# A decoder layer on one core: where RWKV's gates stand between the triangles and the scan

## The chip, the core and the metric

One core of a Trainium2 chip runs the whole program. TensorE (PE) multiplies, VectorE (DVE), ScalarE (ACT) and GpSimd (POOL) work element by element, SyncE (SP) issues most DMAs, and GpSimd issues the gathers of the experts' rows. The metric is the device time of one execution in microseconds.

## The reference, cut to what matters

One layer of a hybrid decoder over a prompt of 1024 tokens and over 8 sample tokens: a gated mixer (an SSD branch and an RWKV-7 branch), cross attention over 256 memory tokens, and a lookup of experts (each token dots 128 rows of `expert_u` and sums 128 rows of `expert_v`). The change concerns the mixer, and in it the gate of the RWKV branch:

```python
g = jax.nn.sigmoid(gl) @ p['rwkv_g2']
yr, wkv_new = _rwkv7_scan(rh, heads(decay), kh, vh, -kk, kk * ah, wkv_prev)
...
y_rwkv = (yr + bonus.reshape(b, L, D_RWKV)) * g
gate_ssd, gate_rwkv = jnp.split(jax.nn.sigmoid(gate_raw), 2, axis=-1)
merged = gate_ssd * y_ssd + gate_rwkv * y_rwkv
```

The factor g times gate_rwkv is wanted only when the scan's output of a block of 128 tokens is complete.

## The kernel before

The prompt is done in four fronts of two blocks of 128 tokens; `front(gi)` is the mixer of one of them, and what follows (attention, choice of experts) is `rest`. The experts' rows of a finished front are gathered by GpSimd (L1514), dotted (L1518) and summed (L1570) on VectorE beside the next front, so fronts 1 to 3 share VectorE and the DMA engines with that stream, and front 0 doesn't. In front 0 the memory's keys and values are computed beside the scan instead.

Inside a front: norm, projections, convolution and SSD, RWKV's projections, then four stages that matter here.

- **Triangles**: the scan treats chunks of 64 tokens at once, and needs inverses of triangles of 32 x 32. All of a front lie in one tile, and 31 steps on VectorE (a product, L843, and a sum, L845) invert them. The result is written to memory (`td`, L846) and read back by each chunk in another shape (`tx`, L911).
- **SSD gates** (L849 to 857): four strips of 256 columns of w_in. A strip is, for each block, a group of matmuls against 1 MB of weights (two loads at L256) into a PSUM tile pp.
- **RWKV gates** (L860 to 882): four rounds q, each with such a strip per block, tanh on ScalarE (L870), a matmul with rwkv_g2 into a PSUM tile pc, and their product on VectorE (L874) into gg. The front with the sample rows (front 1) has a third strip per round, and loads 8 rows of the sample's result (yr, L880). Read at L1019.
- **Scan**: for each of the two blocks b and each of its two chunks c, scores (pg, pc, with masks at L928 and L930 and transposes tp at L934), the read-back inverse turned (L912) and used (tp from tx), then px, pu (solution), py (outputs), ps, and the state rst (L992, L993), on which the next chunk's px waits. A front has four chunks, counted 0 to 3 below.

In the source the gates stand between the triangles and the scan. A scheduler orders each engine's instructions ahead of time by what they depend on and by their place in the source, so that the gates run on TensorE while VectorE inverts. Weight tiles come from a pool of five halves of a strip; PSUM has two tiles each for pp, pc and tp. All engines run their list strictly in order.

The sample's own experts (products at L1697, matmuls pv) run beside front 3.

Of the kernel before, what the change touches and what calls it, by code (L numbers as in the profile page):

```python
# [29 lines left out]
MPOS = 2  # L30
# [16 lines left out]
def decode_layer(ctx, tc, I, O):  # L47
# [17 lines left out]
    def t(tag, shape, bufs, dt=F32):  # L65
        uid[0] += 1
        return (we if tag in of_experts else pools.get(tag, pools.get("wd", wk))).tile(shape, dt, tag=tag, name=f"{tag}_{uid[0]}", bufs=bufs)
# [4 lines left out]
    def rowt():  # L72
        return t("U", [P, D], n_u())

    def q3():
        return t("q3", [P, 2, TMAX], NQ3)
# [10 lines left out]
    def k1():  # L87
        return t("k1", [P, 256], NK1)

    def f2():  # L90
        return t("f2", [P, 512], 4)
# [5 lines left out]
    def pp():  # L97
        return pst("pp", 2)
# [7 lines left out]
    def pc():  # L106
        return pst("pc", 2)

    def pv():
        uid[0] += 1  # L110
        return psp.tile([P, D], F32, tag="pv", name=f"pv_{uid[0]}", bufs=1)

    def mm(out, a, b, first=True, last=True):
        T.matmul(out, a, b, start=first, stop=last)  # L114

    def copy(out, in_, scale=None, bias=None):
        if bias is not None:
            S.activation(out, in_, AF.Identity, scale=scale if scale is not None else 1.0, bias=bias)
        else:
            S.activation(out, in_, AF.Copy, scale=scale if scale is not None else 1.0)  # L120
# [74 lines left out]
    c = spots["conv_w"]  # L195
# [57 lines left out]
    def weights(w, c0, n=256, split=False):  # L253
        x = Weights()
        for i in range(2):
            load(x.half[i][:, :, :n], w[i * 512:(i + 1) * 512, c0:c0 + n].rearrange("(k p) c -> p k c", p=P))  # L256
        return parts(x) if split else x
# [73 lines left out]
    def by_token(wt, h, t0, n, p, nw=256):  # L331
        for k in range(8):
            if isinstance(h, Parts):
                three(p[:n, :nw], h.of(k, slice(t0, t0 + n)), wt[k], k == 0, k == 7)
            else:
                mm(p[:n, :nw], h[k // 2][:, k % 2, t0:t0 + n], wt.of(k, slice(0, nw)), k == 0, k == 7)
# [127 lines left out]
    def front(gi):  # L464
# [393 lines left out]


        gg = [[q3().rearrange("p j x -> p (j x)") for _ in range(2)] for _ in range(nb)]  # L860
        for q in range(4):
            qs = slice(q * 256, q * 256 + 256)
            g2 = k1()
            load(g2, I["rwkv_g2"][0, :, qs])
            wt = weights(w_in, GR0 + q * 256, split=sa)
            for b, (t0, n) in enumerate(body):
                p = pp()
                by_token(wt, hT, t0, n, p)
                th = f2()
                S.activation(th[:n, :256], p[:n, :256], AF.Tanh, scale=0.5)  # L870
                p2 = pc()
                if b < nb:
                    mm(p2[:, :256], lor[:, 1, t0:t0 + n], g2)
                    V.scalar_tensor_tensor(gg[b][q // 2][:, (q % 2) * 256:(q % 2) * 256 + 256], th[:, :256], 1.0,  # L874
                                           p2[:, :256], op0=OP.add, op1=OP.mult)
                else:
                    mm(p2[:n, :256], smp["gl"], g2)
                    V.scalar_tensor_tensor(th[:n, :256], th[:n, :256], 1.0, p2[:n, :256], op0=OP.add, op1=OP.mult)
                    gy = f2()
                    load(gy[:n, :256], smp["yr"][:, qs])  # L880
                    V.tensor_tensor(gy[:n, :256], th[:n, :256], gy[:n, :256], op=OP.mult)
                    V.tensor_tensor(mg[nb][:n, qs], mg[nb][:n, qs], gy[:n, :256], op=OP.add)
        if gi == 0 and MPOS == 0:
            memory()
            keys()


        lnw = []
# [5 lines left out]
        def scan(b):  # L894
            yq = [q3().rearrange("p j x -> p (j x)") for _ in range(2)]
            for c in range(2):
# [94 lines left out]
                        mm(ps[sl, ac], E[s][a // 4][:, a % 4, 0:64], uv[:, s, ac])  # L991
                V.tensor_tensor(rst, ps.rearrange("p (a v) -> p a v", a=8), rst, op=OP.add)  # L992
                V.tensor_tensor(rst, rst, wc[:, :, ch_:ch_ + 1].to_broadcast([P, 8, 64]), op=OP.mult)  # L993


            gst = t("gst", [P, 2, 16], 2)
# [211 lines left out]
        if gi in SPLIT and ORDER:  # L1208
            res = []
            for b in range(nb):  # L1210
                scan(b)
                if gi == 0 and b == 0 and MPOS:
                    memory()
                    keys()
                res += rest([b])
        else:
            for b in range(nb):
                scan(b)
                if gi == 0 and b + 1 == MPOS:
                    memory()  # L1220
                    keys()
            if last and ORDER == 0:
                final_states()
            res = [x for b in range(nb) for x in rest([b])] if gi in SPLIT else rest(list(range(nb)))
# [481 lines left out]
    def keys():  # L1706
        for i in range(2):
            x = rowt()
            load(x.rearrange("p (x d) -> p x d", x=8),
                 I["sub_keys"][0].rearrange("h c k d -> k (h c) d")[:, i * 8:i * 8 + 8, :])  # L1710
            p = pv()
            for c in range(8):
                T.transpose(p[:, c * P:(c + 1) * P], x[:, c * P:(c + 1) * P], ident)
            o = t("acc", [P, D], NAC)
            copy(o, p)
            load(kt2_d[i], o.rearrange("p (x k) -> p x k", x=8))
# [9 lines left out]

    late = []
    chosen = front(0)
    sample_recurrences()
    for gi in range(1, len(GROUPS)):  # L1730
        ahead = front(gi)
        z = experts(prompts(chosen), GATHERED[gi - 1])
        late += [x for i, x in enumerate(z) if i not in GATHERED[gi - 1]]
        samples(chosen)
        chosen = ahead
# [71 lines left out]
```

## Time and profile before

| | us |
|---|---|
| timed runs, median of 3 | 4762.22 (4757.62 to 4777.23) |
| the profiled execution | 4803.32, its span 4801.6 |
| VectorE busy | 3656.8 (76%) |
| TensorE busy | 3581.8 (75%) |
| fronts' triangles begin | 308, 1249, 2245, 3276 |
| states of chunks 0 to 3 done (L993), front 0 | 397, 430, 469, 505 |
| the same, front 1 | 1377, 1419, 1464, 1497 |
| the same, front 2 | 2354, 2394, 2439, 2471 |
| the same, front 3 | 3390, 3433, 3478, 3522 |

The profiled execution is 0.86% longer than the median of the timed runs. A busy TensorE is not TensorE at its peak: the granted clock, 1.00 for 2.4 GHz and 0.50 for 1.2 GHz, is a column of its own. The stages' limits are not those of the average, so that windows are cut along the times in the table.

### The profile page before, as it was taken

How to read it: one execution, taken by the hardware profiler on the slowest of the kernel's cores; microseconds unless marked ns; L12 is line 12 of the kernel's file. 1: busy time of each engine (PE TensorE's matmuls, PEld its weight loads, DVE VectorE, ACT ScalarE, POOL GpSimd, SP SyncE). 2: the span in 40 equal slices, each digit the busy share in tenths (PEclk: the TensorE clock that was granted, in tenths of full speed). 3: DMA queues.
4: the chain of work that ended last, by engine and by line, in shares of the span. 5: the costliest groups of instructions: out<-in, count | busy, mean ns of one | idle time of the engine just before them, and what ended most of it. 6: DMA issues, size and time to landing. Idle time of an engine off the chain costs nothing.

```text
span 4801.6 us, 56531 instructions
## 1 busy us (share of the span) xinstructions
PE 3581.8 (75%) x18486; PEld 2721.1 (57%) x18486; DVE 3656.8 (76%) x7730; ACT 1345.3 (28%) x3461; POOL 2456.4 (51%) x2059
## 2 busy tenths in 40 slices
PE   7889865769887786687676953588867964089995
PEld 6778764557565674365555742465655623056663
DVE  4662296998878779988786899877773798786775
ACT  5544322123132221232232311231321222143331
POOL 0000044765657644655566567745563566754444
PEclk9988887889856896888668976688578985589997
DMA  4342589899978997999799897999788888889997
GB/s 121 99 140 62 195 285 324 269 319 347 342 256 301 360 345 255 343 331 340 269 312 337 318 322 246 335 296 331 224 314 284 283 290 272 309 285 364 354 363 266
DMA packets 609102, 1369.20 MB, mean 285 GB/s; under 512 B 86124, under 2 KB 332296, under 8 KB 608800
## 3 DMA queue, kind: packets, MB, share of 16 engines
q0 software_dynamic: 260352, 948.03, 55.8%
q1 hardware_dynamic: 348456, 417.57, 26.2%
q8 instruction: 146, 2.39, 0.2%
q14 instruction: 148, 1.21, 0.1%
HBM read 1335.60 MB, written 29.90 MB: 284 GB/s over the span
## 4 chain that ended last, share of the span: by engine, by line
PE 40%; DVE 29%; DMA 11%; issue 10%; ACT 5%; POOL 4%; SPq 1%; another core or an unknown queue 0%; POOLq 0%; DVEq 0%; ACTq 0%
PE pp L114 21%; PE pc L114 10%; DVE U L1518 8%; DVE acc L1570 4%; PE pv L114 4%; POOL U L1514 4%; DMA U<-in_expert_u_dram,idx 3%; DMA U<-in_expert_v_dram,idx 2%; PE pg L114 2%; DVE q3b L452 2%; DVE vs L1618 1%; PE tp L114 1%; DMA w<-in_w_in_dram 1%; DVE f L581 1%; DVE q3b L455 1%
## 5 line engine op out<-in xcount | busy, mean ns | idle before, releaser
L1514 POOL DMA_INDIRECT U<-in_expert_u_dram,idx x1024 | 1280.9, 1251 | 828.9 <-DVE act L1518 249.4
L1518 DVE CUSTOM_DVE_ANT_0 U<-U,xa 128x1024 f32<-128x1024 f32 x1032 | 1271.1, 1239 | 140.8 <-DMA U<-in_expert_u_dram,idx 132.8
L1514 POOL DMA_INDIRECT U<-in_expert_v_dram,idx x768 | 900.7, 1173 | 751.4 <-DVE act L1518 248.0
L1570 DVE SCALAR_TENSOR_TENSOR acc<-U,cf,acc 128x1024 f32<-128x1024 f32 x656 | 863.5, 1316 | 111.4 <-DMA U<-in_expert_v_dram,idx 102.5
L114 PE MATMUL pp<-qw,w 128*128 128x256 f32 (+2 forms) x2872 | 731.3, 407 | 159.6 <-issue 43.8
L114 PEld LDWEIGHTS pp<-qw,w 128*128 128x128 f32 x2872 | 580.6, 214 | 281.8 <-issue 107.3
L114 PE MATMUL pp<-w,qw 128*128 128x256 f32 (+1 forms) x2528 | 623.0, 400 | 116.8 <-ACT f L856 44.5
L114 PEld LDWEIGHTS pp<-w,qw 128*128 128x128 f32 (+1 forms) x2528 | 477.4, 192 | 242.7 <-ACT f L856 46.9
L114 PE MATMUL pv<-U,dg 128*128 128x512 f32 x448 | 240.8, 669 | 99.1 <-DMA U<-in_expert_v_dram,idx 85.6
L114 PEld LDWEIGHTS pv<-U,dg 128*128 128x128 f32 x448 | 88.8, 209 | 217.5 <-issue 147.6
L114 PE MATMUL pc<-vs,cs 128*128 128x512 f32 x510 | 204.3, 455 | 1.9 <-DVE vs L1648 1.9
L114 PE MATMUL pp<-q,w 128*128 128x128 f32 (+1 forms) x1024 | 187.2, 340 | 4.5 <-DMA w<-in_w_pq_dram 3.3
L123 POOL TENSOR_TENSOR q3b<-q3b,q3b 128x400 f32<-128x400 f32 (+1 forms) x130 | 152.1, 1184 | 55.8 <-DVE q3b L452 53.2
L114 PEld LDWEIGHTS pp<-q,w 128*128 128x128 f32 x1024 | 163.3, 202 | 19.1 <-issue 3.7
L114 PE MATMUL pp<-vs,cs 128*128 128x512 f32 x510 | 172.2, 392 | 0.0
L114 PE MATMUL pc<-rst,q 64*64 64x64 f32 x1024 | 170.5, 305 | 2.2 <-issue 1.2
L114 PE MATMUL pg<-q,q 64*128 64x128 f32 (+1 forms) x384 | 110.8, 447 | 71.6 <-DMA q<-kt_d 33.3
L306 PE MATMUL tp<-ident,g 128*128 128x128 f32 (+1 forms) x296 | 60.8, 340 | 138.0 <-DVE g L1020 50.5
L114 PE MATMUL pc<-g,q 128*64 128x64 f32 x1024 | 140.0, 317 | 23.1 <-issue 16.6
L1648 DVE TENSOR_TENSOR vs<-Vx,vs 128x512 fp32r<-128x512 f32 x170 | 111.7, 688 | 42.1 <-ACT vs L120 35.0
L114 PEld LDWEIGHTS pg<-q,q 64*128 64x128 f32 (+1 forms) x384 | 82.5, 276 | 94.1 <-ACT q L1130 40.1
L306 PEld LDWEIGHTS tp<-ident,g 128*128 128x128 f32 (+1 forms) x296 | 43.2, 179 | 157.7 <-issue 56.2
(506 smaller groups left out, 6336.3 us busy)
## 6 DMA issues: line engine op xcount, KB each, us to landing
w<-in_w_in_dram SPq DMA_DIRECT2D x248, 512.0 KB
Vx<-in_expert_v_dram SPq DMA_DIRECT2D x128, 512.0 KB
w<-in_w_pq_dram SPq DMA_DIRECT2D x80, 512.0 KB
w<-in_w_out_dram SPq DMA_DIRECT2D x40, 512.0 KB
w<-in_w_mq_dram SPq DMA_DIRECT2D x40, 512.0 KB
w<-in_w_mo_dram SPq DMA_DIRECT2D x40, 512.0 KB
U<-in_expert_u_dram,idx POOLq DMA_INDIRECT x1024
U<-in_expert_v_dram,idx POOLq DMA_INDIRECT x768
```

The source lines that it names most:

```text
L114: T.matmul(out, a, b, start=first, stop=last)
L123: G.tensor_tensor(out, a, b, op=op)
L306: T.transpose(p[:, j * P:j * P + n], x[:, c * P:(c + 1) * P], ident[:n, :n])
L452: V.tensor_tensor(oh[:n], iota50[:n, None, :].to_broadcast([n, 8, NCAND]), posf[:n, h, k8].unsqueeze(2).to_broadcast([n, 8, NCAND]), op=OP ...
L455: V.tensor_reduce(idf[:n, h, k8], oh[:n], axis=AX.X, op=OP.add)
L581: V.scalar_tensor_tensor(acc[:, 3 - k:TP], p[:, :TP - 3 + k], cw(k), acc[:, 3 - k:TP], op0=OP.mult, op1=OP.add)
L1514: G.indirect_dma_start(out=dst, out_offset=None, in_=table, in_offset=bass.IndirectOffsetOnAxis(ap=idx, axis=0))
L1518: V.tensor_tensor_reduce(out=u, in0=u, in1=x, scale=1.0, scalar=0.0, op0=OP.mult, op1=OP.add, accum_out=out)
L1570: V.scalar_tensor_tensor(z["acc"], v, cf, z["acc"], op0=OP.mult, op1=OP.add)
L1618: V.tensor_scalar(rb[:, a, :], iota, by[:, 1, t0 + a:t0 + a + 1], by[:, 2, t0 + a:t0 + a + 1], op0=OP.is_equal, op1=OP.mult)
L1648: V.tensor_tensor(vl, v[:, s], vh.bitcast(F32), op=OP.subtract)
```

## The change

The loop over q becomes a function `gate_rwkv(q)`, and scan(0), the scan of the first block, calls it at the end of each of its two chunks: q = 0 and 1 behind chunk 0, q = 2 and 3 behind chunk 1. This holds for all fronts. The removed lines on MPOS did nothing (MPOS is 2).

```diff
--- before.py
+++ after.py
@@ -858,7 +858,7 @@
 
 
         gg = [[q3().rearrange("p j x -> p (j x)") for _ in range(2)] for _ in range(nb)]
-        for q in range(4):
+        def gate_rwkv(q):
             qs = slice(q * 256, q * 256 + 256)
             g2 = k1()
             load(g2, I["rwkv_g2"][0, :, qs])
@@ -880,9 +880,6 @@
                     load(gy[:n, :256], smp["yr"][:, qs])
                     V.tensor_tensor(gy[:n, :256], th[:n, :256], gy[:n, :256], op=OP.mult)
                     V.tensor_tensor(mg[nb][:n, qs], mg[nb][:n, qs], gy[:n, :256], op=OP.add)
-        if gi == 0 and MPOS == 0:
-            memory()
-            keys()
 
 
         lnw = []
@@ -991,6 +988,9 @@
                         mm(ps[sl, ac], E[s][a // 4][:, a % 4, 0:64], uv[:, s, ac])
                 V.tensor_tensor(rst, ps.rearrange("p (a v) -> p a v", a=8), rst, op=OP.add)
                 V.tensor_tensor(rst, rst, wc[:, :, ch_:ch_ + 1].to_broadcast([P, 8, 64]), op=OP.mult)
+                if b == 0:
+                    for q in range(2 * c, 2 * c + 2):
+                        gate_rwkv(q)
 
 
             gst = t("gst", [P, 2, 16], 2)
```

Every instruction before exists after; the lists are in another order. In SP's list of front 2, here around the write of the inverse (td), before (w_in and w_out are weights; w_15110 and w_15111 belong to q = 3):

```order
L256 DMA w_15110<-in_w_in_dram 128x4x256
L256 DMA w_15111<-in_w_in_dram 128x4x256
L256 DMA w_16142<-in_w_out_dram 128x4x256
L256 DMA w_16143<-in_w_out_dram 128x4x256
L256 DMA w_16166<-in_w_out_dram 128x4x256
L256 DMA w_16167<-in_w_out_dram 128x4x256
L256 DMA w_16190<-in_w_out_dram 128x4x256
L846 DMA td_188<-g_2839_14822 128x1024
L911 DMA tx_15150<-td_188 32x16x32 x2
```

and of the change (w_15228, w_15229 belong to q = 0, w_15508, w_15509 to q = 2, w_15542, w_15543 to q = 3):

```order
L256 DMA w_15228<-in_w_in_dram 128x4x256
L256 DMA w_15229<-in_w_in_dram 128x4x256
L256 DMA w_15262<-in_w_in_dram 128x4x256
L256 DMA w_15263<-in_w_in_dram 128x4x256
L256 DMA w_15508<-in_w_in_dram 128x4x256
L256 DMA w_15509<-in_w_in_dram 128x4x256
L256 DMA w_15542<-in_w_in_dram 128x4x256
L846 DMA td_188<-g_2839_14822 128x1024
L908 DMA tx_15014<-td_188 32x16x32 x2
L256 DMA w_15543<-in_w_in_dram 128x4x256
L256 DMA w_16142<-in_w_out_dram 128x4x256
```

The five loads of w_out that stood right ahead of the write stand behind it, and weights of q = 2 and half of q = 3 are what stands ahead.

TensorE, front 2, from the last matmul of ps of chunk 0 (pc_15343, after: pc_15207) to chunk 1's scores (pc_15384, after: pc_15316), before:

```order
L114 MATMUL pc_15343<-g_2924_15247,q_2915_15163 64x64
L114 MATMUL pc_15384<-q_2725_14252,q_2726_14253 128x128
L114 MATMUL pc_15384<-q_2727_14261,q_2728_14262 128x128
L114 MATMUL pc_15384<-q_2760_14423,q_2761_14424 128x128
L114 MATMUL pc_15384<-q_2762_14432,q_2763_14433 128x128
L114 MATMUL pg_15399<-q_2795_14594,q_2796_14595 128x128
```

and of the change (pp_15526 is the second strip of q = 2; pc from k_ and q_2657 is the product with rwkv_g2, two blocks each of q = 0 and q = 1):

```order
L114 MATMUL pc_15207<-g_2888_15111,q_2879_15027 64x64
L114 MATMUL pp_15526<-w_15508,qw_12965 128x256 x2
L114 MATMUL pp_15526<-w_15508,qw_12966 128x256 x2
L114 MATMUL pp_15526<-w_15509,qw_12967 128x256 x2
L114 MATMUL pp_15526<-w_15509,qw_12968 128x256 x2
L114 MATMUL pc_15243<-k_2894_15226,q_2657_13949 128x256
L114 MATMUL pc_15257<-k_2894_15226,q_2657_13949 128x256
L114 MATMUL pc_15277<-k_2903_15260,q_2657_13949 128x256
L931 MATMUL tp_15347<-ident,q_2796_14595 128x128
L931 MATMUL tp_15347<-ident,q_2798_14604 128x128
L931 MATMUL tp_15347<-ident,q_2831_14766 128x128
L931 MATMUL tp_15347<-ident,q_2833_14775 128x128
```

A strip and four gate products (the fourth behind these rows) now stand between the two chunks. The strips of q = 0 stay ahead of the scan, the two of q = 1 stand where the inverse is read back, the first of q = 2 between pu and py of chunk 0; chunk 1 has the same with q = 3. In front 1, with three strips a round, three stand at the end of chunk 0, one and a quarter inside chunk 1, and two and three quarters at its end; none is left between the triangles and chunk 0's scores.

VectorE, end of front 0's triangles, before (q_501 and q_503 are gg; L247 is the norm of the memory):

```order
L845 TENSOR_TENSOR g_458_2873<-g_458_2873,f_459_2874 128x2x30
L874 SCALAR_TENSOR_TENSOR q_501_3214<-f_551_3478,pc_3480 128x256
L843 TENSOR_TENSOR f_459_2874<-g_457_2872,g_458_2873 128x31
L247 RECIPROCAL ssm_4481<-ssm_4481 128x1
L845 TENSOR_TENSOR g_458_2873<-g_458_2873,f_459_2874 128x31
L874 SCALAR_TENSOR_TENSOR q_503_3216<-f_554_3508,pc_3510 128x256
L928 TENSOR_TENSOR q_563_3531<-pg_3535,maskg 128x4x64
L930 TENSOR_TENSOR f_562_3530<-pg_3535,maskg 64x256
```

and of the change (U_3809, w_3879 and U_3883 are weights split into two parts, which only front 0 does; L909 to L990 are L912 to L993 of before):

```order
L845 TENSOR_TENSOR g_458_2873<-g_458_2873,f_459_2874 128x2x30
L843 TENSOR_TENSOR f_459_2874<-g_457_2872,g_458_2873 128x31
L845 TENSOR_TENSOR g_458_2873<-g_458_2873,f_459_2874 128x31
L909 STREAM_TRANSPOSE tx_3225<-tx_3225 32x1024
L292 TENSOR_TENSOR U_3809<-w_3800,U_3807 128x1024
L909 STREAM_TRANSPOSE tx_3585<-tx_3585 32x1024
L292 TENSOR_TENSOR w_3879<-w_3873,U_3877 128x1024
L989 TENSOR_TENSOR rst<-pc_3418,rst 128x512
L990 TENSOR_TENSOR rst<-rst,wc_1534 128x512
L292 TENSOR_TENSOR U_3883<-w_3874,U_3881 128x1024
L874 SCALAR_TENSOR_TENSOR q_500_3213<-f_537_3476,pc_3478 128x256
L874 SCALAR_TENSOR_TENSOR q_502_3215<-f_540_3506,pc_3508 128x256
```

The products of gates and the norm are gone from the last steps, and the gates follow the state of chunk 0; the masks of chunk 0 stand ahead of the last steps. Of the splits at L292, 11 stand in front 0's triangles before and 8 after; of the masks, none before and eight after.

VectorE's experts, L1518 and L1570 together, counted in the two lists by stage, before and after ("rest" is all between the scan of the front before and these triangles; the tail is what follows the state of chunk 3 up to the last merge, L1020):

| | rest | triangles | chunk 0 | chunk 1 | chunk 2 | chunk 3 | tail |
|---|---|---|---|---|---|---|---|
| front 1 | 225, 218 | 32, 39 | 20, 18 | 22, 28 | 20, 28 | 17, 17 | 17, 16 |
| front 2 | 306, 316 | 24, 33 | 25, 22 | 19, 20 | 23, 25 | 17, 10 | 17, 14 |
| front 3 | 348, 342 | 24, 14 | 15, 8 | 18, 19 | 19, 21 | 18, 18 | 12, 12 |

The gates' operations on VectorE (L874, and for the sample rows L878, L881, L882) stand, by the same count, before: 7 in the triangles and 1 in chunk 0 (front 1: 8 and 12); after: 4 in chunk 1 and 4 in chunk 2 (front 1: 10 and 10). Behind front 3's scan the counts are the same. The sample's experts (L1697) stand in chunk 0 of front 3 before, and in its triangles after. In front 0 the memory's matmuls that stood inside the scan stand behind it as far as the gates take their places.

## Rows read from the trace of the kernel before

**Rows 1.** Windows of stages named below: columns are named in the first line.

```profile
core 0: us, PE busy (x) PEld busy (x) DVE busy (x) ACT busy (x) POOL busy (x), PEclk, DMA share, GB/s
530.00:575.00 45.00, 32.34 (x210) 27.47 (x208) 7.24 (x23) 14.12 (x38) 0.41 (x2) 0.89 0.81 275
1249.00:1312.00 63.00, 58.23 (x248) 38.75 (x249) 62.27 (x133) 6.09 (x17) 44.82 (x33) 0.93 1.00 367
1312.00:1377.00 65.00, 55.48 (x398) 42.60 (x396) 36.45 (x61) 18.46 (x47) 24.53 (x22) 0.66 0.76 259
1377.00:1419.00 42.00, 37.04 (x306) 29.87 (x304) 36.54 (x45) 12.26 (x42) 31.24 (x26) 0.50 0.76 255
1419.00:1464.00 45.00, 37.58 (x323) 31.13 (x323) 37.05 (x60) 21.59 (x69) 28.26 (x22) 0.50 0.71 236
2298.00:2354.00 56.00, 30.98 (x313) 25.31 (x312) 39.59 (x52) 14.11 (x39) 32.88 (x29) 0.60 0.75 261
2354.00:2394.00 40.00, 30.93 (x296) 24.96 (x296) 31.95 (x43) 13.74 (x48) 24.59 (x22) 0.58 0.76 254
2394.00:2439.00 45.00, 36.26 (x306) 29.75 (x307) 41.12 (x62) 19.02 (x59) 31.50 (x25) 0.50 0.82 267
2439.00:2470.00 31.00, 26.58 (x284) 21.56 (x283) 24.66 (x35) 8.49 (x24) 21.62 (x18) 0.72 0.86 284
3329.00:3390.00 61.00, 55.17 (x369) 35.34 (x368) 34.07 (x46) 18.10 (x46) 27.43 (x26) 0.67 0.74 242
```

**Rows 2.** Groups of instructions: count, busy us, mean ns; or count, ns min/median/max.

```profile
L1518 DVE CUSTOM_DVE_ANT_0 U<-U,xa 128x1024 f32<-128x1024 f32 x1032 | 1271.1, 1239 | 140.8 <-DMA U<-in_expert_u_dram,idx 132.8
...
L1570 DVE SCALAR_TENSOR_TENSOR acc<-U,cf,acc 128x1024 f32<-128x1024 f32 x656 | 863.5, 1316 | 111.4 <-DMA U<-in_expert_v_dram,idx 102.5
...
L874 DVE SCALAR_TENSOR_TENSOR q<-f,pc x32: 406/414/422, 330.5 to 3330.7; 128x256 f32<-128x256 f32 x32
...
L292 DVE TENSOR_TENSOR w<-w,U x31: 1215/1225/1227, 25.4 to 340.1; 128x1024 fp32r<-128x1024 f32 x31
...
L928 DVE TENSOR_TENSOR q<-pg,maskg 128x256 f32<-128x256 f32 x3 | 1.3, 422 | 9.4 <-PE pc L114 9.3
```

**Rows 3.** Timeline of VectorE, end of front 0's triangles: start us, us, [idle before <-releaser].

```profile
351.41 0.42 DVE L874 SCALAR_TENSOR_TENSOR q<-f,pc 128x256 f32<-128x256 f32 x1 [1.90 <-ACT f L870]
...
353.02 0.16 DVE L247 RECIPROCAL ssm<-ssm 128x1 f32<-128x1 f32 x1 [1.09 <-ACT ssm L246]
```

**Rows 4.** Timeline of SP, the inverse's write and read, fronts 0 and 1.

```profile
353.34 0.34 SPq L846 DMA_DIRECT2D td<-g  x1
...
356.38 0.87 SPq L911 DMA_DIRECT2D tx<-td  x2
...
1312.15 0.33 SPq L846 DMA_DIRECT2D td<-g  x1
...
1326.46 1.95 SPq L911 DMA_DIRECT2D tx<-td  x2
```

**Rows 5.** Chain that ended last, 1290 to 1385: start us, us, what.

```profile
by line: PE pc L114 19.2%; DMA f<-yr_d 18.0%; issue 12.1%; DVE acc L1570 11.8%; DMA tx<-td 6.5%; DVE U L1518 4.3%; PE pv L114 4.0%; PE tp L114 3.7%; PE pg L114 3.3%; DVE g L845 3.0%; DVE f L843 2.9%; DVE q L874 2.1%; DVE acc L1535 1.5%; DVE
```

**Rows 6.** Waits of TensorE, 2298 to 2358: total us, times, longest us.

```profile
PE tp L114 <- DMA tx<-td: 11.2, 1, 11.2
PE pc L114 <- issue: 10.5, 3, 7.7
```

**Rows 7.** Waits of VectorE, chunk 0 of front 3.

```profile
DVE dgs L1697 <- PE pv L114: 13.0, 5, 5.0
```

**Rows 8.** Timeline of TensorE, strips of gates (pp): start us, us.

```profile
1321.06 3.62 PE L114 MATMUL pp<-w,qw 128*128 128x256 f32 x16
...
2274.78 3.56 PE L114 MATMUL pp<-w,qw 128*128 128x256 f32 x8
```

**Rows 9.** Windows inside chunk 0 of front 0.

```profile
384.00:387.00 3.00, 3.00 (x25) 2.19 (x25) 0.00 (x0) 0.00 (x0) 0.00 (x0) 1.00 0.00 0
387.00:396.00 9.00, 9.00 (x71) 6.94 (x70) 0.70 (x2) 1.39 (x5) 0.00 (x0) 0.51 0.01 2
```


## The prediction

> **What bounds the kernel now.** I read the windows by stage first [rows 1], then the single operations that move [rows 2], then the waits at both ends of the triangles and inside the scans [rows 3 to 7], and last the prices on TensorE [rows 8, 9]. The change moves work and adds none, so the question is only where an engine stands idle and whether it will stand idle longer.
>
> In the triangles of front 1 VectorE is busy for 62.27 of 63 us, with TensorE at 58.23 and the DMA engines at a share of 1.00 [rows 1]: that stage is bound by VectorE. The scan behind it is not: its first three chunks last 65, 42 and 45 us with VectorE at 36.45, 36.54 and 37.05, so 28.6, 5.5 and 8.0 us of it are idle, while the granted clock is 0.66, 0.50 and 0.50, which is TensorE on its low level for much or all of the time [rows 1]. Front 2 has 16.4, 8.1, 3.9 and 6.3 idle in its four chunks, front 3 has 26.9 in its first [rows 1]. A chunk is a chain of small matmuls and copies; the experts' dots and sums of the front before (L1518, L1570) fill what they can.
>
> Their number is fixed. By the table of counts ahead, fronts 1 to 3 hold 1238 of them before and 1238 after, and behind front 3's scan nothing has moved. So a stage that gets longer because dots were put into it returns that time in a stage that loses them, and what the change is worth in fronts 1 to 3 is **the change of VectorE's idle time**. In front 0 there are no dots; there I go by the path.
>
> **Front 0.** Out of the triangles go seven gate products at 0.414 us and three splits at 1.22; in come eight mask products at 0.42 [rows 2]: 2.9 + 3.7 - 3.4 = 3.2 us less. The last steps also wait 1.90 us for the tanh of a gate, which leaves, and 1.09 us for the norm of the memory [rows 3], which the order has later: 3.0 less. Since the scores of chunk 0 are now masked before the inverse ends, up to 5 us of its head go as well; I take 2. That is -8. Against it, six of the eight strips run inside the scan of front 0, and push the memory's matmuls behind it. At the nearest row for a strip, 3.62 us [rows 8], they are 21.7 us, and between 530 and 575 us TensorE has 45 - 32.3 = 12.7 idle to take them [rows 1]; at most 9 are left, and since much of the memory is off the path I take 3. Front 0: **-5**, ends -11 and +6.
>
> **Front 1.** Before, four strips of 3.62 us [rows 8] lie between the end of the triangles and chunk 0, and three loads of sample rows come between the write of the inverse and its read; one of them takes 17.13 us [rows 5]. The read goes out 14.3 us after the write (1312.15 to 1326.46), against 3.0 us in front 0 (353.34 to 356.38) [rows 4]. After, the two stand next to each other on SP but for half the norm's weights, and w_out is loaded later. I let chunk 0 shrink from 65 to 51 us (14.3 - 3.0 = 11.3 from the round trip, 3 from the strips). It loses two dots at about 1.28 (between the two rows' means) and twelve gate operations at 0.41 [rows 2]: VectorE's work goes from 36.5 to 29.0, idle from 28.6 to 22: -6.5. Chunks 1 and 2 get 14 more dots (17.9) and 20 gate operations (8.2): work 73.6 + 26.1 = 99.7 [rows 1, 2]. Their length, 87 us, grows by 5.75 strips at 3.62 (20.8), by cold starts (below) 5, by two rounds of gate products, which alternate between TensorE and VectorE through two buffers of PSUM, 4, less 6 for matmuls that then find the clock up: about 111. Idle 11.6 against 13.4: -2. In sum **-8**, ends -15 (all waits in these chunks filled) and +8 (chunk 0 no shorter than 58).
>
> **Front 2.** The order puts the two strips of q=1 into the hole in which TensorE waits 11.2 us for the inverse, and the first strip of q=2 into one of 7.7 us between the chunk's solution and its outputs [rows 6]: nothing for either. Chunk 0: from 56 to 50 us, since w_out's five loads no longer stand right ahead of the write on SP; three dots less, work 39.6 to 35.8, idle 16.4 to 14.2: -2. At the end of chunk 0 the second strip of q=2 and four gate products come ahead of the next chunk's scores: 3.6 to 5.3 us for the strip (half of it at the low clock: eight matmuls in 3.56 us instead of sixteen in 3.62 [rows 8]), 2 for the products, less 2 for the clock behind the strip: +4.5 to chunk 1. With one dot and four products more in it (2.9) its idle time grows by 1.6; chunk 2 alike, with two dots, by 0.3. In the last chunk seven of 17 dots are gone (-9 of work [rows 1, 2]); were its length unchanged, that were 9 more idle, and with VectorE as its bound none: +6, nearer to the first end, because 6.3 are idle there already. Sum **+6**, ends 0 and +14.
>
> **Front 3.** Its first chunk has VectorE waiting 13.0 us for matmuls of the sample's experts [rows 7]. The order moves these into the triangles, so the chunk shrinks by some 16 us; but it also loses seven dots and the experts' work, so its idle time stays about where it is: 0. The waits partly reappear in the triangles: +2 of 0 to 5. Chunks 1 and 2 as in front 2: +2. **+4**, ends -4 and +9.
>
> **Sum**: -5 - 8 + 6 + 4 = **-3 us**. On the profiled execution of 4803.3 us that is 4800; it lies 0.86% above the median of the timed runs, 4762.2, so the forecast is 4762.2 - 3, about **4759**, its own range 4740 to 4780. What a measurement can tell from no change is about 0.5%, 24 us.
>
> **Clock, row and rule.** In front 0, where the memory's matmuls lie between the parts of a chunk, the granted clock behind them is 1.00 from 384 to 387 us and 0.51 from 387 to 396, while the chunk's own matmuls keep TensorE busy throughout [rows 9]: the high clock (2.4 GHz) that such a strip brings does not last the chunk. Three of those twelve microseconds ran at twice the speed; of this I took 2 us per strip ahead of a chunk's matmuls. The Trainium skill, "TensorE: Matmul & The Clock Gate", section "HAM oscillation — how this bites in real kernels", says that idle gaps between groups of matmuls throw TensorE back to its low clock, so that each group starts cold. By that page alone strips in the gaps would keep a whole chunk warm, and the sum would be the first rival's; the row speaks against it, since TensorE was busy without a gap when its clock fell.
>
> **Rivals.** *A gain*: the chunks start earlier and the strips hold the clock up. For it: the round trip of 14.3 us and the wait of 11.2 [rows 4, 6], and DMA shares of 0.71 to 0.82 in the scans' first three chunks against 1.00 in the triangles [rows 1], so that weights moved there delay no gather. Its price is the lower ends of fronts 0, 1 and 3 with front 2 at its own: -11 - 15 + 0 - 4 = -30, and some 1.5 us more per chunk with gates in the six of fronts 1 to 3, -9: about **4724**. Against it: chunk 0 has fewer dots to fill with, so time saved there is partly idle time moved.
>
> *A loss*: the gates stand ahead of the next chunk's scores on TensorE in program order. Place: the ends of chunks 0 and 1 of all four fronts. Price: the upper ends, +6 + 8 + 14 + 9 = +37: **4799**. It decides if a strip there costs its cold price (7 us when all sixteen run as the eight at 2274.78 [rows 8]) and VectorE has no dot ready; 8 such strips at 3.4 over their warm price are 27 of the 37. For it: the clock of 0.50 in just these chunks. Against it: the dots that the order puts into front 1.
>
> *Not what it says*: two strips of each front stay in the triangles, and dots take the room that the others leave, so that the inverse ends no earlier: **4762**. The order shows both; only where the dots would have waited elsewhere does it count.
>
> **How the numbers follow.** Forecast 0.40, gain 0.30, loss 0.24, not what it says 0.06. Faster by over 0.5% is the gain, 0.30; slower by over 0.5% the loss, 0.24; within 0.5% the other two, 0.46. The range takes more than half of both rivals in: it ends 6 us below the time of the gain and 7 us above that of the loss, which leaves some 0.1 of the 0.30 and 0.08 of the 0.24 outside.
>
> **What would show it.** Right: front 0's write of the inverse near 347 us; the read within 6 us of the write in fronts 1 and 2; chunk 0 shorter by 14, 6 and 16 us in fronts 1 to 3; chunks 1 and 2 longer by about 24 together in front 1 and 4 to 5 each in fronts 2 and 3; VectorE's idle time over the fronts' scans and triangles unchanged within 10 us. Wrong: a granted clock above 0.7 through chunks 1 and 2, chunks that grow by 8 us each with VectorE idle, or a stage A whose length changes by more than its dots.

## The result: 0.6% slower

Nine runs of each kernel in turn on the same chips: 4798.2 us median (4780.6 to 4807.3) against 4765.5 (4749.3 to 4781.4), a ratio of 1.006 with a 95% interval of 1.004 to 1.008. The forecast was 4759 within a range of 4718 to 4806: the time is in the range and right at the rival called a loss (4799), but the change moved it upward by 33 us, where the forecast was 3 us down and "no change" the likeliest case.

One thing had to be cleared first. The profiled execution of the kernel before was 38 us longer than its median, and the changed kernel's is at its own median (4799.4), so the two traces differ by 4 us only. A second profile of the kernel before (first experiment) took 4757.5 us; front 2's chunk 0 lasts 48 us in it, not 57, and front 3's chunk 3 34, not 44. The wait of 11.2 us in [rows 6] was 8.7. All comparisons below are with that second profile, where no other is named.

The spans of both, cut at the same steps (the triangles' first, and the last merge of a front, L1020); "idle" is VectorE's:

| | before: us, idle | after: us, idle |
|---|---|---|
| front 0 | 524.1, 269.3 | 524.3, 268.6 |
| ahead of front 1 | 720.6, 134.5 | 738.8, 172.9 |
| front 1, triangles to last merge | 271.3, 46.4 | 302.3, 57.9 |
| ahead of front 2 | 716.8, 105.3 | 740.3, 112.7 |
| front 2 | 241.7, 24.8 | 246.4, 32.5 |
| ahead of front 3 | 779.7, 136.8 | 771.5, 133.9 |
| front 3 | 249.2, 47.5 | 221.0, 39.9 |
| all behind | 1252.3, 338.4 | 1252.8, 336.0 |
| sum | 4755.8, 1102.8 | 4797.4, 1154.6 |

Front 0 itself is as long as before, front 3 is 28 us shorter, and the loss lies in front 1 (31 us) and in the stages ahead of fronts 1 and 2 (18 and 24).

**Ahead of front 1.** Windows of 116 us behind front 0, after and then before (columns as in [rows 1]), and VectorE's waits in the stage, 524 to 760 us, after and then before:

```profile
524.00:640.00 116.00, 93.25 (x537) 81.65 (x536) 14.04 (x42) 27.61 (x72) 0.41 (x2) 0.88 0.65 208
```

```profile
524.00:640.00 116.00, 93.72 (x580) 83.36 (x579) 51.71 (x112) 32.22 (x79) 18.65 (x9) 0.87 0.82 281
```

```profile
DVE sx L1126 <- PE pg L114: 59.0, 2, 52.7
```

```profile
DVE sx L1126 <- PE pg L114: 20.4, 3, 10.9
```

TensorE and its clock are alike; VectorE does 14.0 us of work for 51.7. It stands for 52.7 us in front of the attention's first scores (L1126), which need the memory's keys and come 59 us behind front 0's last merge, for 44 before. What VectorE did ahead of them before is the head of the sample rows' recurrences (from L1274 on). It is a few us of work, but the recurrences' long products (L1320) hang on it. The timeline of VectorE shows that this head stands behind the scores now, after and then before:

```profile
583.67 0.69 DVE L1126 TENSOR_REDUCE sx<-pg 128x2 f32<-128x512 f32 x1 [52.73 <-PE pg L114]
...
591.84 0.26 DVE L1274 TENSOR_TENSOR xa<-sraw,cols 128x96 f32<-128x96 f32 x1
```

```profile
540.12 0.26 DVE L1274 TENSOR_TENSOR xa<-sraw,cols 128x96 f32<-128x96 f32 x1
...
568.50 0.69 DVE L1126 TENSOR_REDUCE sx<-pg 128x2 f32<-128x512 f32 x1 [10.92 <-PE pg L114]
```

So the long products begin at 639 us for 584 and run beside the choice of experts. The first block's choice (L456) is made at 709 us for 664, and the first gather starts at 761 for 706. Of these 55 us the stage loses 18 in the end.

**The triangles of fronts 1 and 2.** Windows of the changed kernel at their ends, then the kernel before, front 1:

```profile
1320.00:1339.00 19.00, 0.00 (x0) 0.00 (x0) 18.97 (x36) 0.00 (x0) 14.38 (x14) 0.50 0.90 324
...
2340.00:2369.00 29.00, 0.21 (x1) 0.00 (x0) 28.62 (x57) 0.24 (x1) 21.18 (x17) 0.50 0.85 296
```

```profile
1288.00:1308.00 20.00, 20.00 (x92) 15.01 (x91) 19.76 (x47) 1.90 (x5) 16.36 (x11) 1.00 0.96 332
```

TensorE, which before did the gates' strips here at its high clock for nothing, now stands idle for 19 and 29 us while VectorE works on through dots: the triangles of front 1 take 76 us for 63, those of front 2 64 for 53. The strips come later, between the chunks. Chunk 1 of fronts 1, 2 and 3, after and then before:

```profile
1393.00:1450.00 57.00, 56.56 (x416) 40.99 (x415) 44.86 (x67) 13.42 (x34) 40.16 (x31) 0.79 0.79 263
...
2414.00:2454.00 40.00, 35.63 (x352) 28.44 (x350) 34.97 (x52) 12.63 (x34) 27.05 (x23) 0.91 0.91 304
...
3405.00:3445.00 40.00, 38.92 (x367) 31.35 (x365) 35.96 (x40) 11.09 (x30) 27.02 (x23) 0.87 0.87 296
```

```profile
1377.00:1418.00 41.00, 34.88 (x300) 28.59 (x300) 35.70 (x46) 13.66 (x51) 32.06 (x24) 0.50 0.74 244
...
2334.00:2373.00 39.00, 29.26 (x284) 23.65 (x284) 31.22 (x42) 12.46 (x45) 24.28 (x22) 0.56 0.76 261
...
3369.00:3406.00 37.00, 34.51 (x302) 28.64 (x300) 30.17 (x32) 12.20 (x41) 22.63 (x21) 0.50 0.73 246
```

In fronts 2 and 3 the chunk takes 60-odd more matmul records in 0 and 2.5 us more (39.9 us for 39.9, 39.5 for 37.0, cut at the states). Strips and gate products take 14.9 and 15.7 us of TensorE in these windows; the other matmuls take 20.7 us for 29.3 and 23.2 for 34.5, with the granted clock at 0.91 and 0.87 for 0.56 and 0.50. In front 1 the chunk takes 16 us more, at 0.79. That the strips cost so little holds for this list alone: in kernels below, with front 0 unchanged, chunk 1 of fronts 2 and 3, where they are changed, takes 46 to 49 us at 0.71 to 0.81.

### The profile page after: what moved, and what is told of

Same layout as the page of the kernel before. It is cut to its first block, busy times and chain, and to the rows that moved or that the text cites. A ratio compares the mean times of both kernels' runs of the same rounds, so it can differ in the third digit from the quotient of the medians.

```text
span 4797.4 us, 56496 instructions
## 1 busy us (share of the span) xinstructions
PE 3546.3 (74%) x18486; PEld 2689.6 (56%) x18486; DVE 3642.7 (76%) x7730; ACT 1350.1 (28%) x3466; POOL 2524.0 (53%) x2059
## 4 chain that ended last, share of the span: by engine, by line
PE 38%; DVE 29%; DMA 14%; issue 8%; ACT 5%; POOL 4%; SPq 1%; POOLq 0%; DVEq 0%; ACTq 0%
PE pp L114 21%; PE pc L114 9%; DVE U L1518 8%; DVE acc L1570 4%; POOL U L1514 4%; DMA U<-in_expert_u_dram,idx 3%; PE pv L114 3%; DMA U<-in_expert_v_dram,idx 2%; DMA w<-in_w_in_dram 2%; PE pg L114 2%; DVE q3b L452 2%; DMA q<-kt_d 1%; PE tp L114 1%; DVE vs L1618 1%; DVE q3b L455 1%
## 5 line engine op out<-in xcount | busy, mean ns | idle before, releaser
L1514 POOL DMA_INDIRECT U<-in_expert_u_dram,idx x1024 | 1313.4, 1283 | 795.6 <-DVE act L1518 254.6
L1518 DVE CUSTOM_DVE_ANT_0 U<-U,xa 128x1024 f32<-128x1024 f32 x1032 | 1276.1, 1244 | 169.8 <-DMA U<-in_expert_u_dram,idx 165.6
L1514 POOL DMA_INDIRECT U<-in_expert_v_dram,idx x768 | 931.1, 1212 | 660.0 <-DVE act L1518 193.5
L1570 DVE SCALAR_TENSOR_TENSOR acc<-U,cf,acc 128x1024 f32<-128x1024 f32 x656 | 853.7, 1301 | 129.3 <-DMA U<-in_expert_v_dram,idx 117.4
L114 PE MATMUL pp<-w,qw 128*128 128x256 f32 (+1 forms) x2528 | 641.4, 407 | 122.9 <-ACT f L856 45.0
L114 PE MATMUL pc<-rst,q 64*64 64x64 f32 x1024 | 158.0, 286 | 2.3 <-DVE rst L990 2.1
L114 PE MATMUL pc<-g,q 128*64 128x64 f32 x1024 | 130.0, 304 | 2.8 <-ACT g L120 2.8
L120 ACT ACTIVATE vs<-Vx 128x512 fp32r<-128x512 f32 x170 | 100.7, 620 | 90.6 <-PE pp L114 82.5
```

The costliest lines, as they stand in the source:

```text
L1514: G.indirect_dma_start(out=dst, out_offset=None, in_=table, in_offset=bass.IndirectOffsetOnAxis(ap=idx, axis=0))
L1518: V.tensor_tensor_reduce(out=u, in0=u, in1=x, scale=1.0, scalar=0.0, op0=OP.mult, op1=OP.add, accum_out=out)
L1570: V.scalar_tensor_tensor(z["acc"], v, cf, z["acc"], op0=OP.mult, op1=OP.add)
```

## The experiments

Ratios are to the kernel before, timed on the same chip beside each run (its median lay at 4761 to 4765 us on some chips, 4795 and 4809 on two others).

**The kernel before, a second profile.** No edit.

> The kernel before, unchanged, for a second profile of it: its first profiled execution took 4803 us, 38 above the median of its timed runs, so a difference of stages between two single profiles may belong to the execution and not to the change. Both theories expect 4750 to 4780 us. What it decides is where the 38 us lay: if in front 3's scan and triangles (193 us in the first profile up to its last merge from the end of the triangles, 48 more in the stage before), the gain of about 25 us of idle time that the changed kernel shows there is no gain of the change.

Measured 4757.5 us, span 4755.8. The two profiles are 46 us apart, spread: 10 in front 2's chunk 0, 16 in chunks 1 and 3 of front 3, 6 ahead of front 1, the rest in smaller pieces. Part of what front 3 seemed to gain was therefore none. Front 3's chunk 3 took 41 to 46 us in every profile from the two chips with the longer medians and 29 to 34 in those from the other chips, so that some of this may belong to the chip.

**Front 0 alone, fronts 1 to 3 alone, and the memory earlier.** The second kernel has (1, 2, 3) in both places; the third is the changed kernel with the last edit alone.

```diff
+        if gi not in (0,):
+            for q in range(4):
+                gate_rwkv(q)
...
-                if b == 0:
+                if b == 0 and gi in (0,):
...
-MPOS = 2
+MPOS = 1
```

> The gates between the chunks in front 0 alone; in fronts 1 to 3 they stand before the scan, as before. Theory M (memory): front 0's strips push the keys and values of the memory behind the scan, the attention and the choice of experts of front 0 end later, the first gather starts some 50 us later (704 us before, 761 in the changed kernel), and VectorE stands idle for some 30 us more ahead of front 1: ratio 1.005 to 1.008, all or more of the loss. Theory C (chunk ends): the loss is made where the strips stand ahead of the next chunk in fronts 1 to 3, and here nothing is lost: ratio 0.999 to 1.002.

> The gates between the chunks in fronts 1 to 3 alone; front 0 as before. Theory M: the first gather is back near 704 us and the stage ahead of front 1 as before; ratio 0.996 to 1.001. Theory C: the whole loss is here, ratio 1.004 to 1.008, with front 1's chunks 1 and 2 at 57 and 60 us as in the changed kernel (41 and 45 before).

> The changed kernel with the memory's keys and values written in the source between the two scans of front 0 and not behind the second, so that they stand ahead of the second scan. Theory M: a good part of the loss comes back, the first gather by 10 us or more earlier than 761; ratio to before 0.998 to 1.004. Theory C: no change against the changed kernel, 1.004 to 1.008. If the memory's place costs the scan of front 0 what it gives to the choice of experts, the ratio stays too, with chunks 2 and 3 of front 0 longer by over 10 us.

Front 0 alone: 1.0036 (1.0021 to 1.0052), 16 us. VectorE's waits ahead of front 1 are those of the changed kernel:

```profile
DVE sx L1129 <- PE pg L114: 60.1, 2, 53.9
```

Fronts 1 to 3 alone: 1.0097 (1.0073 to 1.0121), more than the whole change, with the stage ahead of front 1 as before (720.7 us). So both theories hold a part, and the parts do not add. The memory earlier: 1.0131 (1.0107 to 1.0155), worse. The stage ahead of front 1 falls to 700.7 us, but chunks 2 and 3 of front 0 take 61 us each, for 44 and 36 in the changed kernel; theory M's place was right, and this was no cure: the stage ahead of front 1 gains 38 us and front 0 pays 42, as the last sentence expected. Not expected was that the ratio rose; against the changed kernel's profile fronts 2 and 3 and the stage ahead of front 2 are longer as well (by 11, 16 and 7 us), and why is open.

**Which of fronts 1 to 3.** The same edit with (1,), (2, 3) and (3,).

> The gates between the chunks in front 1 alone, where each round has a third strip. Theory C (chunk ends): 5.75 strips stand at the ends of chunks 0 and 1; those chunks take 53 and 59 us as with fronts 1 to 3 together (41 and 42 before), chunk 0 gives back 15: some 10 to 15 us lost in front 1, ratio 1.002 to 1.004. Theory D (dots): front 1 itself loses no idle time of VectorE (183 us with fronts 1 to 3, 181 before), since the dots that it brings forward fill it; but 14 to 16 dots are then missing later, and where the list has none left VectorE waits: idle time ahead of front 2 goes from 105 to 115 to 123, ratio 1.002 to 1.004 as well. What tells them apart is the place: front 1's own idle time over 190 for C, 178 to 186 with over 115 behind it for D.

> The gates between the chunks in fronts 2 and 3 alone. Both theories: the rest of the 46 us that fronts 1 to 3 lost together. Theory C: chunks 1 and 2 of each longer by 4 to 6 us, ratio 1.003 to 1.005, and VectorE's idle time rises inside these chunks. Theory D: the chunks' idle time stays within 3 us, and it rises in chunk 0 of front 3 and ahead of it (155 and 36.7 us with fronts 1 to 3, 137 and 26.7 before), ratio 1.004 to 1.007.

> The gates between the chunks in front 3 alone. Theory C: two boundaries at 4 to 6 us, against chunk 0 that no longer holds the sample's experts: ratio 0.999 to 1.001. Theory D: as long as no dots are brought forward from fronts 1 and 2, front 3 has dots enough for chunk 0, and its end comes earlier: ratio 0.996 to 0.999, the version that would beat both kernels. If the loss of fronts 2 and 3 is all in front 3: 1.003 or more.

Front 1 alone: 1.0062 (1.0040 to 1.0085). Fronts 2 and 3: 1.0003 (0.9981 to 1.0025). Front 3: 1.0018 (1.0000 to 1.0036). Most of the later fronts' loss is front 1's, more than the 1.002 to 1.004 of both theories, and fronts 2 and 3 lose less than either said; none of these versions beats the kernel before. Front 1's idle time was 196 us with the stage ahead of it, on theory C's side of 190, but 8 of it lay ahead of the gates; behind it, ahead of front 2, it was 126, theory D's sign, against 114 in the run of front 3 alone on the same chip.

**Short strips, extra strips.** In the first two kernels (front 1 alone changed, front 0 alone changed; gi == 0 in the second) the gates' strips do 2 of 8 steps; which experts are chosen then differs, their number doesn't. In the third the kernel before gets strips behind L993 whose results nobody uses. The kernel before ran once more for a profile.

```diff
-                by_token(wt, hT, t0, n, p)
+                by_token(wt, hT, t0, n, p, ks=(0, 7) if gi == 1 else range(8))
...
+                if b == 0 and gi == 1:
+                    for _ in range(3):
+                        p = pp()
+                        for k in range(8):
+                            mm(p[:, :256], hT[k // 2][:, k % 2, 0:P], rst.rearrange("p a v -> p (a v)")[:, 0:256],
+                               k == 0, k == 7)
```

> As with front 1 alone changed, but each of its twelve strips of RWKV gates does 2 of its 8 steps over the inner dimension (its gates are wrong; loads, tanh, products and places stay). Theory C' (the chain of the scan): what the change costs is the time of the strips on TensorE between the chunks, wherever it is paid; with strips of 0.9 us for 3.6, chunks 1 and 2 of front 1 together fall from 115 us to 90 or less, VectorE's idle time behind front 1 is back at that of before, and the loss is gone: ratio 0.995 to 1.000, against 1.006 with whole strips. Theory D' (the list): gates taken out of the triangles let the list pull dots forward, which then lack behind front 1, however short the strips are: ratio 1.003 to 1.007, idle time ahead of front 2 still 10 us or more above that of before.

> As with front 0 alone changed, but each of its eight strips of RWKV gates does 2 of its 8 steps over the inner dimension (its gates are wrong). Theory M (memory displaced by the strips' time on TensorE): six strips of about 2.8 us become 0.7, the memory is done some 12 us earlier, and most of the loss of 0.36% comes back: ratio 0.998 to 1.002, the wait of VectorE for the attention's scores ahead of front 1 back from 54 us to under 30. Rival (order alone): the list puts the memory behind the scan whatever the strips take: ratio 1.003 to 1.005, the wait still near 50.

> The kernel before, its gates where they were, with three more strips of matmuls (results unused) behind chunk 0 and three behind chunk 1 of front 1, each of 16 matmuls of the shape of a gate's strip, on the new state, so that they can't run earlier. Theory C': 6 x 3.6 to 5 us more on the chain, 22 to 30 us; chunks 1 and 2 of front 1 longer by 11 to 15 each, filled in part with dots, which then lack ahead of front 2: ratio 1.003 to 1.006. Theory D': as no gate left the triangles, dots stay where they were: chunks longer, but the ratio 1.000 to 1.002.

> The kernel before once more, for a profile from the chip of the three others: VectorE's idle time in front 1 (181 us on another chip), ahead of front 2 (105) and in fronts 2 and 3 (130, 184) to compare theirs with. Expected within 15 us of these sums on every theory.

The third profile of the kernel before took 4762.3 us; its four sums of idle time are 184, 108, 131 and 180 us, all within 4 of those named. Front 1 with short strips: 1.0057 (1.0037 to 1.0077), as with whole ones, with 41 dots and sums in the triangles and 72 us for them. Chunks 1 and 2 still take 102 us together (82 in that third profile; theory C' said 90 or less). The strips' time on TensorE is not the bulk of the cost. Front 0 with short strips: 1.0025 (1.0010 to 1.0039), between the ranges of theory and rival and not clearly less than 1.0036, and the wait is as long as ever:

```profile
DVE sx L1129 <- PE pg L114: 62.1, 2, 55.8
```

It is the memory's place in the list, not the strips' duration. Six extra strips: 1.0032 (1.0016 to 1.0048), 15 us, the lower end of what theory C' gave: chunks 1 and 2 of front 1 longer by 5.4 and 5.7 (theory C' said 11 to 15). So strips on the chain cost something too, without any gate being moved.

**The transfers kept, and fewer rounds moved.** First, in the kernel with front 1 alone changed, the gates' weights are loaded a second time at the old place, with eight narrow matmuls that read them; beside it front 1 alone again; then only the last round of front 1 behind chunk 0 (the diff's second part), and the last two (range(2), and rounds 2 and 3 behind the chunk).

```diff
+        if gi == 1:
+            for q in range(4):
+                wt = weights(w_in, GR0 + q * 256)
+                p = pp()
+                for i in range(2):
+                    mm(p[:, :8], hT[2 * i][:, 0, 0:P], wt.half[i][:, 0, 0:8], i == 0, i == 1)
...
+        for q in range(4) if gi != 1 else range(3):
+            gate_rwkv(q)
...
+                if gi == 1 and b == 0 and c == 0:
+                    gate_rwkv(3)
```

> As with front 1 alone changed, but at the gates' old place the same eight halves of weights are loaded once more (4 MB, with eight narrow matmuls that only read a corner of them), so that the list has as many transfers beside the triangles as before. In the list the sums L1570 in front 1's triangles go from 20 back to 15 (16 before). Theory D' (transfers that leave the triangles let the list pull dots forward; they lack later): triangles back from 72 to 63 us, idle time ahead of front 2 back below 112, and most of the loss gone although 4 MB more are moved: ratio 0.999 to 1.003, at least 0.3% under the kernel with front 1 changed. Rival (the gates' work in the chunks, on whatever engine): triangles back at 63, but the loss stays or grows by the 11 us of transfers: 1.005 to 1.009.

> Front 1 alone changed, again, on the chip of the run with loads kept, since its first run was on another chip: both theories 1.004 to 1.008, triangles of front 1 near 72 us with 41 of the experts' operations in them.

> Front 1 alone, and of its four rounds only the last (q = 3, three strips) behind chunk 0; the other three stay beside the triangles. Before, four strips run over the end of the triangles, so that TensorE has no idle time there to lose; the list holds 16 sums L1570 in the triangles, as before. Theory D': no loss, ratio 0.997 to 1.001, with triangles at 63 us, chunk 0 shorter by 8 to 12 and chunk 1 longer by as much. Rival (any strip behind a chunk costs its time): ratio 1.002 to 1.004, 11 us.

> Front 1 alone, rounds q = 2 and 3 (six strips) behind chunk 0, the first two beside the triangles. The list holds 16 sums L1570 in the triangles, as before. Theory D': the triangles stay at 63 us; TensorE idles for some 4 us at their end, so a loss of 4 to 10 us at most: ratio 0.999 to 1.003. Rival (any strip behind a chunk costs its time): 22 us, ratio 1.004 to 1.006, as with all four rounds.

With the transfers kept the ratio is 1.0020 (1.0005 to 1.0035), without them 1.0065 (1.0046 to 1.0084) on the same chip. The groups of dots and sums on VectorE in front 1's triangles, before, front 1 alone, and with the transfers kept:

```profile
L1518 DVE CUSTOM_DVE_ANT_0 U<-U,xa 128x1024 f32<-128x1024 f32 x17 | 20.7, 1219 | 0.4 <-DMA U<-in_expert_u_dram,idx 0.4
L1570 DVE SCALAR_TENSOR_TENSOR acc<-U,cf,acc 128x1024 f32<-128x1024 f32 x16 | 20.4, 1277 | 0.0
```

```profile
L1573 DVE SCALAR_TENSOR_TENSOR acc<-U,cf,acc 128x1024 f32<-128x1024 f32 x21 | 26.9, 1280 | 0.0
L1521 DVE CUSTOM_DVE_ANT_0 U<-U,xa 128x1024 f32<-128x1024 f32 x21 | 25.6, 1218 | 0.3 <-DMA U<-in_expert_u_dram,idx 0.3
```

```profile
L1527 DVE CUSTOM_DVE_ANT_0 U<-U,xa 128x1024 f32<-128x1024 f32 x16 | 19.5, 1220 | 0.4 <-DMA U<-in_expert_u_dram,idx 0.4
L1579 DVE SCALAR_TENSOR_TENSOR acc<-U,cf,acc 128x1024 f32<-128x1024 f32 x15 | 19.2, 1277 | 0.0
```

33, 42 and 31, and the triangles take 63, 72 and 61 us (the windows take in one more than counts by list and by start do). The dots follow the transfers: when the gates' weights leave the triangles, the list fills the room with gathers, and VectorE, which bounds the stage, gets nine dots and sums more to do ahead of the inverse. One place where these lack is seen 200 to 240 us into the stage ahead of front 3, before (the third profile) and then front 1 alone:

```profile
2677.40:2717.40 40.00, 40.00 (x203) 32.71 (x202) 37.95 (x194) 12.45 (x36) 12.99 (x14) 1.00 0.97 320
```

```profile
2712.60:2752.60 40.00, 40.00 (x203) 32.54 (x202) 28.49 (x186) 16.19 (x43) 3.21 (x4) 1.00 0.40 132
```

TensorE does the same 203 matmuls; GpSimd has 4 instructions for 14, the DMA engines 132 GB/s for 320, and VectorE, with no dot at all in these 40 us for 15 before, is idle for 11.5 us for 2.0. The next choice of experts isn't made yet, and the old one is used up: no gather stands between 2698 and 2762 us, and VectorE makes the choice. With the transfers kept there are 12 dots in this stretch, and 1.1 us idle. The sum over that stage hides it (134.7 us idle for 136.3); ahead of front 2 idle time is 119.0 us for 107.9, and 113.6 with the transfers kept (theory D' said below 112). Where all of the loss of front 1 is paid is thus shown in part only.

The last round alone costs 1.0018 (0.9999 to 1.0037), two rounds 1.0035 (1.0017 to 1.0052), with triangles at 63 us as in the list. Theory D' wanted 1.001 or less and 1.003 or less, the rival 1.002 to 1.004 and 1.004 to 1.006; the runs lie between. One round behind a chunk costs about 8 us (0 to 18) with no dot pulled forward, near the 11 us of its three strips of 3.6.

## Why the prediction failed, point by point

- **The sum's rule.** It counted VectorE's idle time inside triangles and scans, taking it that a stage that loses dots gets shorter by as much. Over the whole program idle time does tell the loss: +51.8 us of it for a span longer by 41.6. But the triangles and scans of fronts 1 to 3 together went from 118.7 us of idle time to 130.3: +11.6, for +2 in the sum (the third profile of the kernel before has 110.6, so that single profiles differ by 8 here). The stages between the fronts went from 376.6 to 419.5: +42.9. 38.4 of these lie ahead of front 1, where the sum had 3 us for the memory; 7.4 lie ahead of front 2, where it had no term, and ahead of front 3 it is 2.9 less. The term that failed most is the memory's, and the next is front 1's -8.
- **Front 0, -5.** The triangles' part was right: they are 6.8 us shorter, and the write of the inverse is at 351 us (354 to 355 before; 347 forecast), as they began 3 us later. Chunk 0 is shorter by 13, chunks 1 and 2 longer by 12 and 6, so the scan's end is where it was. The term for the memory ("at most 9 are left, and since much of the memory is off the path I take 3") failed: VectorE is idle for 38 us more behind it and the stage is 18 longer. I priced TensorE's time there; the price is that the memory's keys, put behind the scan by the list, come 15 us later, and that VectorE waits for them in its own list with the head of the recurrences behind that wait. Shown by the two kernels with front 0 alone (wait 54 and 56 us, with whole and with short strips; 16 and 12 us lost).
- **Front 1, -8, ends -15 and +8.** Its idle time rose by 11.5. Chunk 0 came down to 54 us, near the forecast (51), chunks 1 and 2 went to 117 together (111). Not forecast: the triangles, 13 us longer, which I had at no change. The table of counts showed seven dots more there; I booked them as work moved, though VectorE's time there is the chain's. 5.2 us of the 13 are waits for gathered rows (L1570) that the kernels with front 0 unchanged don't have: their triangles take 72 us with 0.7 idle.
- **Front 2, +6**, measured +7.7, but by luck: chunk 0 gave +6.1 for -2 and chunk 1 -2.8 for +1.6. **Front 3, +4**, measured -7.6. In front 3 the sample's experts left chunk 0 (35 us for 62), as forecast, and 2.9 us of their waits reappeared in the triangles (+2 was forecast); chunk 0's idle time, forecast to stay, fell from 26.7 to 18.7. Alone these two fronts are worth nothing (1.0003).
- **The round trip of the inverse**: 8.9 us in front 1 for 14.3 [rows 4], and 7.9 in front 2; within 6 was forecast. In the second profile it was 11.4 in both fronts before, so the base of the term was too high as well. SP's timeline of the changed kernel:

```profile
1339.47 0.38 SPq L846 DMA_DIRECT2D td<-g  x1
...
1348.34 0.86 SPq L908 DMA_DIRECT2D tx<-td  x2
```

- **The clock**: above 0.7 in chunk 1 of three fronts, which I had named as a sign against me, and 0.63, 0.55 and 0.54 in their chunk 2. In chunk 1, which holds two strips and the gate products, it goes with strips that are nearly free in fronts 2 and 3; chunk 2, with one strip at its head, takes 47 and 46 us there for 42 and 44. The Trainium skill ("TensorE: Matmul & The Clock Gate", section "HAM oscillation — how this bites in real kernels") says that idle gaps between groups of matmuls throw TensorE back to its low clock. What I had drawn from it, that strips in the gaps would keep a whole chunk warm, agrees with 0.91 and 0.87 in chunk 1 and not with chunk 2; my reading of [rows 9] held in chunk 2 and was too narrow for chunk 1. It gave no gain, since chunk 1 wasn't shorter for it.
- **The loss rival** had the time, 4799, by luck: its +37 was made of other terms, cold strips at chunk ends in the main. The sixteen matmuls of a strip at the end of chunk 0 took 5.0 and 4.3 us in fronts 2 and 3, not the 7 of its price, and with strips a quarter as long the loss of front 1 stayed. That work behind a chunk costs something is right (15 us for six extra strips, about 8 for one round).

**What stays open.** The parts don't add: front 0 (0.36%) and front 1 (0.62 to 0.65%) with nothing for fronts 2 and 3 make 1.0%, as fronts 1 to 3 alone do (0.97%), and the whole change is 0.60%. Each kernel has a list of its own, and I have not found what in the whole list gives 17 us back, or 35 if front 0's 0.36% is added to the 0.97%. Nor is it settled why one round costs its strips' time behind a chunk while short strips save nothing: a round also brings products on VectorE and loads, and short strips leave 42 dots in the triangles. Moving the memory to the gates' old place in front 0, beside the triangles, might have kept it ahead of the scan; it wasn't tried.

## What to carry to other kernels

When work leaves a stage that another engine bounds, ask what the scheduler will put into the room: here loads of weights left, gathers came, and their dots lengthened the very chain that the stage is bound by. Count idle time over the whole program and not only over the stages that the change names: filler that is used early can be missing later, as in the 40 us without a dot above. And look at each in-order list for what now stands behind an instruction that waits: 53 us of VectorE went to one wait, and a few us of independent work that stood in front of it before, the head of a long chain, came 52 us later for it.

## What was not expected of the hardware

With wide matmuls between the narrow ones of a chunk the granted clock was 0.87 to 0.91 over a whole chunk of 40 us, where it had been 0.50 to 0.56 (windows above); 352 matmul records then took 35.6 us of TensorE, and 284 had taken 29.3. In the chunk behind, with one wide group at its head, it was 0.55 and 0.54. When the loads of the gates' weights left front 1's triangles, the DMA engines' share there fell from 1.00 [rows 1] only to 0.91 over these 76 us: gathers took the room.
